# Hybrid decoder trunk: another order for the planned work behind the attention, from a planner that takes VectorE and GpSimd to share a port

## The chip, the cores and the metric

One core of a Trainium2 chip. The time is device microseconds of one execution. TensorE (PE) does the matmuls and the transposes, VectorE (DVE), ScalarE (ACT) and GpSimd (POOL) the rest; SyncE (SP) issues most loads and stores. Each engine runs its own queue in order and waits on semaphores of the others.

## The reference

One layer on x of 1024 tokens by 1024 channels, all in float32:

```python
h = rms_norm(x, norm1_g)
q, k, v, glu_a, glu_b = split(h @ w_in)          # 512 channels each
attn = stick_breaking_attention(norm(q), norm(k), v)   # 8 heads of 64
c = silu(layer_norm(causal_depthwise_conv(glu_a * sigmoid(glu_b))))   # width 31
x = x + concat([attn, c]) @ w_out
h = rms_norm(x, norm2_g)
gate, val = split(h @ w_up)                      # 2816 channels each
x = x + (silu(causal_depthwise_conv3(gate)) * val) @ w_down
```

## The kernel before

A float32 operand is split in two: a high part rounded to fp32r and a low part, the difference. A product is three matmuls per 128 channels: high by high, high by low, low by high (mm3, lines 289 to 291). Making an operand so takes a cast (ACT) and a subtraction (DVE or POOL).

The kernel has four parts. The first, some 450 us, is the input projection, the conv branch and the attention, with the conv's share of the output projection (op, lines 1200 to 1231) strewn between the attention's matmuls. The second, which the change rewrites, is the rest of the output projection, the second norm and the preparation of the up projection, 450 to 534 us. Then come the up projection (22 blocks of 128 channels of gate and of value) and the down projection.

The up projection uses a block scheme with seven products instead of eight. It treats tokens 0 to 511 and 512 to 1023, and channels 0 to 511 and 512 to 1023, as a 2 by 2 matrix of blocks: 11, 21 (first half of the tokens), 22, and sums of blocks T1 to T4, each in a high and a low part (B, names b11, b21, b22 and bT1 to bT4). The weights are treated alike: a11, a12, a22 and sums S1 to S4 (names a and aS).

In the second part there are eight tiles of 128 tokens, taken in the order 0, 4, 1, 5, 2, 6, 3, 7. For a tile, the steps are (function tokens, from line 1318):

- m: the attention's output of the tile in two parts, on ACT and DVE or POOL (L1332 to L1340).
- two products opa of twelve matmuls each, of 512 output channels (mm3), and each one's add to x on DVE (L1353); x is stored for the down projection.
- the sum of squares on ACT (L1363), its root on POOL (rstd, L280 and L281), and h, the normalized row, in two halves on DVE (L1371).
- two groups of four transposes of h on PE (h2T, L1379).
- for tiles 0 to 3 the copies raws and the blocks 11 and 21; for tiles 4 to 7 the differences t1 to t4 against the tile four before, the block 22, and T1 to T4. A block's part is a cast on ACT (L1391) and a subtraction on DVE or POOL (L1392).

The operands of the first up block (function first_operands, L1500 to L1511) are made at the same time; its weights are rawu. When all this is there, the up products run (up, from line 1531).

The order of parts one and two comes from a planner (class Plan, line 46): every step is an Op with a cost in ns per engine that may run it, a key (a due time) and its predecessors. Plan.run emits in a loop the step that could start first: a step whose key is at most 1 above the lowest open key is ranked by its start less PATIENCE, then by its key. The engine queues are tied to that order. Parts three and four, and the first operands' successors, are ordered by the framework's scheduler, which may set instructions of part three between planned ones. Parts one and two are two plans with the same rules.

In the second part's plan h has key + 0.5, the transposes + 0.7, all blocks + 1.0, and everything else the tile's own number; the first operands come from key FIRST = 7.0.

Of the kernel before, what the change touches and what calls it, by code (L numbers as in the profile page):

```python
# [34 lines left out]
ORDERED = (mybir.EngineType.PE, mybir.EngineType.DVE, mybir.EngineType.Activation, mybir.EngineType.Pool)  # L35
HORIZON, PATIENCE = 3.0, 200
AHEAD_Z, AHEAD_SCAN = 1.7, 0.9
QK_FROM, QK_TO = -3.0, 7.0
CONV_FROM, CONV_TO = 7.0, 31.0
EARLY = 4.0  # L40
W_SHIFT = 0.5
WA_FROM = 30.5
FIRST = 7.0
N_DN = 20


class Plan:
# [8 lines left out]
    class Op:  # L56
        __slots__ = ("cost", "emit", "key", "after", "takes", "end", "engine", "n", "kb")

# [21 lines left out]
    def add(self, cost, *args):  # L80
        if not isinstance(cost, dict):
            cost, args = {cost: args[0]}, (lambda eng, f=args[1]: f(),) + args[2:]
        op = Plan.Op()
        op.cost, op.emit, op.key = cost, args[0], args[1]
        op.after = list(args[2]) if len(args) > 2 else []
        op.takes = list(args[3]) if len(args) > 3 else []
        op.end, op.engine, op.n, op.kb = None, None, len(self.ops), 512
        self.ops.append(op)
        return op
# [17 lines left out]
    def run(self, busy):  # L107
# [12 lines left out]
        left = {id(t): len(set(o.n for o in t.users)) for t in self.tokens}  # L120
        done, dma = 0, 0.0
        main = sorted(self.ops, key=lambda op: op.key)
        low = 0
        while done < len(self.ops):
# [4 lines left out]
            for op in ready:  # L129
# [7 lines left out]
                for e, cost in op.cost.items():  # L137
                    r = room
                    for o in op.after:
                        r = max(r, o.end + (0 if o.engine == e else Plan.POOL_HAND_OVER if e == "POOL" else Plan.HAND_OVER)  # L140
                                + (170 if o.engine == "PE" and e != "PE" else 0))
                    start = max(r, at[e])
                    if e == "SP":
                        start = max(start, dma - 2000)
                    if mine is None or start + cost < mine[0]:
                        mine = (start + cost, e, cost, start)
# [11 lines left out]
            op.end, op.engine = start + cost, e  # L158
            at[e] = (start + 60) if e == "SP" else op.end - over[e]
            if e == "SP":  # L160
                dma = max(dma, start) + op.kb * 2.6
            op.emit(e)
# [14 lines left out]
def kernel(  # L177
# [1135 lines left out]

    ops_done = []

    raws = {}

    def tokens(t, key):
# [10 lines left out]
        def m_high():  # L1329
# [5 lines left out]
        adds = []  # L1335
        a = add("ACT", 250, m_high, key, [], [mr])
        b = [add({"DVE": 260, "POOL": 460}, lambda eng: (nc.vector if eng == "DVE" else nc.gpsimd).tensor_tensor(
            d["m"][:, 1, 3], attn[1][:, tok], f32(d["m"][:, 0, 3]), op=ALU.subtract), key, [a])]
        a = add("ACT", 480, lambda: nc.scalar.copy(d["m"][:, 0, :3], attn[0][:, :, tok]), key, [a])
        b += [add({"DVE": 560, "POOL": 1000}, lambda eng: (nc.vector if eng == "DVE" else nc.gpsimd).tensor_tensor(  # L1340
            d["m"][:, 1, :3], attn[0][:, :, tok], f32(d["m"][:, 0, :3]), op=ALU.subtract), key, [a])]
        for nn in range(2):
# [9 lines left out]
            ops_done.append(m)  # L1352
            f = add("DVE", 690, lambda nn=nn, cols=cols: nc.vector.tensor_tensor(d["x"][:, cols], d["ps", nn], d["x"][:, cols], op=ALU.add), key, [m, xl])  # L1353
            mr.users += [m]
# [9 lines left out]

        c = add("ACT", 1100, square, key + 0.5, adds, [hr, r])
        f = add("POOL", 750, lambda: rstd(d["rs"], d["sq"], 1.0 / D), key + 0.5, [c])
        b = []
        for nn in range(2):
            cols = slice(nn * 512, (nn + 1) * 512)
            z = plan.token("z")  # L1370
            f = add("DVE", 690, lambda nn=nn, cols=cols: nc.vector.scalar_tensor_tensor(  # L1371
                d["h"][:, cols], d["x"][:, cols], d["rs"], g2[1 + nn], op0=ALU.mult, op1=ALU.mult), key + 0.5, [f] + g2_ready)
            r.users += [f]
# [6 lines left out]

            m = add("PE", 440, turn, key + 0.7, [f], [z])
            hr.users += [m]
# [3 lines left out]
        ends = []  # L1386
        key += 1.0
        either = {"DVE": 700, "POOL": 1330}

        def both(name, src, after, lows, raw=None):  # L1390
            a = add("ACT", 600, lambda: nc.scalar.copy(B[name][0][where], src()), key, after)  # L1391
            e = add(lows, lambda eng: (nc.vector if eng == "DVE" else nc.gpsimd).tensor_tensor(  # L1392
                B[name][1][where], (raw or src)(), f32(B[name][0][where]), op=sub), key, [a] + (copies if raw else []))
            ends.append(e)
            return [a, e]

        if t < NT // 2:
# [9 lines left out]
            for nn, (m, z) in enumerate(b):  # L1407
                z.users += [copies[nn]] + both(("11", "21")[nn], lambda nn=nn: d["b", nn], [m], {"POOL": 1330}, lambda nn=nn: raws[t][:, nn])[:1]
            raws["ready", t] = vr, copies, ends
# [14 lines left out]
        z2.users += [d2, d3] + both("22", lambda: d["b", 1], [m2], {"DVE": 690})  # L1424
        d4 = add("POOL", 1330, lambda: nc.gpsimd.tensor_tensor(d["t4"], d["t4"], d["t2"], op=sub), key, [d2] + before)
        both("T2", lambda: d["t2"], [d2], either)
        both("T1", lambda: d["t1"], [d1], either)
        both("T3", lambda: d["t3"], [d3], either)
        both("T4", lambda: d["t4"], [d4], either)
        vr.users += ends + [d4]  # L1430
# [39 lines left out]

    for n, t in enumerate((0, 4, 1, 5, 2, 6, 3, 7)):
        tokens(t, float(n))
    A = {}

    def first_operands(key):
# [19 lines left out]
        def both(name, of, after, k):  # L1495
            def high():
                t = (op.tile([P, 2, 4, P], F32R, tag="m", name=f"a{name}_0", bufs=1) if name == "22" else
                     whl([P, 2, 4, P], F32R, f"a{name}_0"))
# [3 lines left out]

            a = add("ACT", 620, high, key + k, after + ops_done)
            return [a, add({"DVE": 700, "POOL": 1330}, lambda eng: (nc.vector if eng == "DVE" else nc.gpsimd).tensor_tensor(
                A[name][1], src(of), f32(A[name][0]), op=ALU.subtract), key + k, [a])]

        def total(dst, x, y, op_, after, k):
# [4 lines left out]

            return [add({"DVE": 700, "POOL": 1330}, emit, key + k, after)]

# [9 lines left out]
        s4 = total("a12", "a12", "a11", ALU.subtract, s2 + e12, 0.5)  # L1524
        both("S4", "a12", s4, 0.5)

    first_operands(FIRST)
# [3 lines left out]
    def up(f, A):  # L1531
        def product(a, b):
            ps = (pso.tile([P, 512], F32, tag="bank", name=f"u{f}_{a}") if a in ("11", "12") else
                  psz.tile([P, 512], F32, tag="z", name=f"u{f}_{a}"))
            (ah, al), (bh, bl) = A[a], B[b]
            for k in range(4):
                mm3(ps, ah[:, k, :], al[:, k, :], bh[:, k, :], bl[:, k, :], k == 0, k == 3)
            return ps

# [195 lines left out]
```

## Time and profile before

| what | us |
|---|---|
| three runs | 1159.65, 1164.59, 1164.76 (median 1164.59) |
| profiled execution | 1164.32 |
| its span, first to last instruction | 1162.3 |
| PE busy | 1115.9 |
| DVE, ACT, POOL busy | 908.5, 649.6, 605.9 |
| mean granted clock of PE | 0.985 |

A row of the timeline holds start, duration, engine, line, operation, output and inputs with their sizes, the count of merged instructions, and in brackets the idle time ahead of it with what ended it. A group's row holds busy time and the mean of one in ns. A row of waits holds the sum, the count and the longest. A window's row holds its length, then for PE, weight loads, DVE, ACT and POOL the busy time and the instructions, the granted clock as a share, the share of DMA time and GB/s.

### The profile page before, as it was taken

The page shows a single profiled execution, that of the slowest core. Times are in us where ns is not written, and L with a number is a line of the kernel's source. Part 1 is how long each engine was busy: PE and PEld are TensorE (multiplying, and loading weights), DVE is VectorE, ACT ScalarE, POOL GpSimd, SP SyncE. Part 2 cuts the span into 40 slices and gives each one's busy share as a digit, 9 for nine tenths or more (in the row PEclk, how much of TensorE's full clock was granted, in tenths as well). Part 3 has the DMA queues.
Part 4 walks back from the last instruction along what each step waited for, and adds up shares of the span by engine and source line. Part 5 has one row for each costly group of instructions (what it writes and reads, how often), then busy time and mean ns, then how long its engine had stood idle before and what let it go on. Part 6 is the DMA issues. An engine that isn't in the chain of part 4 may idle for free.

```text
span 1162.3 us, 15965 instructions
## 1 busy us (share of the span) xinstructions
PE 1115.9 (96%) x5639; PEld 934.8 (80%) x5639; DVE 908.5 (78%) x1215; ACT 649.6 (56%) x1338; POOL 605.9 (52%) x516
## 2 busy tenths in 40 slices
PE   7999999988899998879999999999999999999998
PEld 5888899867788886668888888888888877888887
DVE  5399966569989887778798777777677689887886
ACT  6255698697777785543344343434333475766670
POOL 5077747567676653454433332233313176877880
PEclk8999999999999999979999999999999999999999
DMA  8011203121933105332422322222222462144303
GB/s 275 19 56 37 61 14 82 47 97 52 284 122 118 55 37 192 116 127 55 127 91 81 101 72 91 73 91 73 91 88 75 134 247 81 65 145 145 127 19 145
DMA packets 108637, 116.48 MB, mean 100 GB/s; under 512 B 20782, under 2 KB 88590, under 8 KB 108558
## 3 DMA queue, kind: packets, MB, share of 16 engines
q1 hardware_dynamic: 108414, 114.95, 30.3%
q8 instruction: 44, 0.72, 0.2%
q10 hardware_dynamic: 144, 0.52, 0.1%
q14 instruction: 35, 0.29, 0.1%
HBM read 82.95 MB, written 28.31 MB: 96 GB/s over the span
## 4 chain that ended last, share of the span: by engine, by line
PE 83%; DVE 7%; ACT 3%; DMA 3%; issue 1%; POOL 1%; SPq 0%; DVEq 0%; ACTq 0%
PE dn L1694 15%; PE u_S L291 7%; PE u_S L289 7%; PE u_S L290 7%; PE u L290 5%; PE u L291 5%; PE u L289 5%; PE po L1120 3%; PE wT L1092 2%; PE v L290 1%; PE v L289 1%; PE v L291 1%; PE glu_b L289 1%; PE glu_b L290 1%; PE glu_a L289 1%
## 5 line engine op out<-in xcount | busy, mean ns | idle before, releaser
L1694 PE MATMUL dn<-wd,wd 128*128 128x512 f32 x924 | 214.2, 393 | 4.3 <-DVE c L1697 2.9
L1694 PEld LDWEIGHTS dn<-wd,wd 128*128 128x128 f32 x924 | 173.7, 189 | 44.7 <-DVE c L1697 5.3
L1697 DVE TENSOR_TENSOR c<-dn,c 128x512 f32<-128x512 f32 x144 | 95.5, 683 | 17.7 <-PE dn L1694 17.3
L1601 ACT CAST wd<-rawd 128x512 fp32r<-128x512 f32 x154 | 87.4, 618 | 36.3 <-DMA rawd<-act_d 11.7
L1071 POOL TENSOR_TENSOR wt<-wt,nb 128x128 f32<-128x128 f32 (+3 forms) x64 | 78.2, 1223 | 50.0 <-DVE nb L1068 34.8
L291 PE MATMUL u_S<-bT,aS 128*128 128x512 f32 x264 | 102.8, 389 | 0.0
L290 PE MATMUL u_S<-bT,aS 128*128 128x512 f32 x264 | 102.7, 389 | 0.0
L289 PE MATMUL u_S<-bT,aS 128*128 128x512 f32 x264 | 102.5, 389 | 0.0
L1068 DVE TENSOR_TENSOR_SCAN nb<-nb,one 128x128 f32<-128x128 f32 (+3 forms) x64 | 85.4, 1345 | 8.6 <-ACT nb L1049 8.4
L285 ACT CAST aS<-rawu 128x512 fp32r<-128x512 f32 x63 | 38.8, 620 | 94.7 <-PE u_S L291 64.8
L1602 DVE TENSOR_TENSOR wd<-whole,wd 128x512 fp32r<-128x512 f32 x110 | 73.9, 684 | 16.7 <-ACT wd L1601 12.9
L1600 ACT COPY whole<-rawd 128x512 f32<-128x512 f32 x110 | 63.2, 584 | 36.6 <-DMA rawd<-in_w_down_dram 19.6
L1460 POOL TENSOR_TENSOR s<-rawu 128x512 f32<-128x512 f32 x21 | 30.8, 1466 | 98.6 <-DMA rawu<-in_w_up_dram 97.3
L1466 POOL TENSOR_TENSOR rawu<-rawu 128x512 f32<-128x512 f32 x21 | 29.0, 1380 | 81.7 <-DVE a L286 81.7
L289 PE MATMUL u<-b,a 128*128 128x512 f32 x176 | 69.9, 398 | 0.4 <-ACT b L1391 0.4
L290 PE MATMUL u<-b,a 128*128 128x512 f32 x176 | 69.7, 396 | 0.1
L291 PE MATMUL u<-b,a 128*128 128x512 f32 x176 | 69.5, 395 | 0.0
L1602 POOL TENSOR_TENSOR wd<-rawd,wd 128x512 fp32r<-128x512 f32 x44 | 57.4, 1322 | 12.1 <-ACT wd L1601 12.1
L285 ACT CAST a<-rawu 128x512 fp32r<-128x512 f32 x63 | 38.9, 621 | 44.1 <-PE u_S L291 30.7
L1555 DVE SCALAR_TENSOR_TENSOR y<-gv,cols_a,y 128x1023 f32<-128x1023 f32 (+1 forms) x44 | 57.0, 1296 | 7.8 <-ACT y L1553 7.7
L286 DVE TENSOR_TENSOR aS<-rawu,aS 128x512 fp32r<-128x512 f32 x63 | 53.5, 851 | 8.3 <-ACT aS L285 8.0
L291 PEld LDWEIGHTS u_S<-bT,aS 128*128 128x128 f32 x264 | 49.6, 188 | 10.6 <-DVE aS L286 0.4
(311 smaller groups left out, 3343.3 us busy)
## 6 DMA issues: line engine op xcount, KB each, us to landing
rawu<-in_w_up_dram SPq DMA_DIRECT2D x44, 512.0 KB
act_d<-y SPq DMA_DIRECT2D x22, 512.0 KB
rawd<-act_d SPq DMA_DIRECT2D x22, 512.0 KB
rawd<-in_w_down_dram SPq DMA_DIRECT2D x22, 512.0 KB
rawo<-in_w_out_dram SPq DMA_DIRECT2D x8, 512.0 KB
m<-conv_d SPq DMA_DIRECT2D x16, 256.0 KB
xt<-in_x_dram SPq DMA_DIRECT2D x8, 512.0 KB
x_part<-xt SPq DMA_DIRECT2D x8, 512.0 KB
```

What stands on the lines that cost most here:

```text
L285: nc.scalar.copy(hi, src)
L289: nc.tensor.matmul(ps, a_hi, b_hi, start=first, stop=False)
L290: nc.tensor.matmul(ps, a_hi, b_lo, start=False, stop=False)
L291: nc.tensor.matmul(ps, a_lo, b_hi, start=False, stop=last)
L1068: nc.vector.tensor_tensor_scan(rev, rev, ones_of[0][:, :w], 0.0, op0=ALU.mult, op1=ALU.add)
L1071: nc.gpsimd.tensor_tensor(d["wt"][:, :w], d["wt"][:, :w], d["nb"][:, o + 1:S + 1], op=ALU.mult)
L1555: nc.vector.scalar_tensor_tensor(y[:, j:], g[:, :S - j], par("fw", (KF - 1 - j) * NF + f), y[:, j:], op0=ALU.mult, op1=ALU.add)
L1600: nc.scalar.copy(whole, src)
L1601: nc.scalar.copy(t[:, 0], src)
L1602: lo_engine.tensor_tensor(t[:, 1], whole, f32(t[:, 0]), op=ALU.subtract)
L1694: nc.tensor.matmul(ps, a[:, tok], b, start=first and m == 0, stop=last and m == 2, skip_group_check=True)
L1697: nc.vector.tensor_tensor(sums[c][s], ps, sums[c][s], op=ALU.add)
```

## The change

Four things, all in the planner or in what it is given.

1. Keys of the second part. The m step moves to the tile's number - 0.5, the adds to - 0.8, the norm to + 0.4; blocks stay at + 1.0, and the sums T1 to T4 with the difference t4 go to + 2.2. The first operands' key is 7.7.
2. The planner's rules, for both plans. PATIENCE is 150. A POOL step that starts while DVE holds the port that the planner takes them to share, or a step with two SBUF operands on DVE (marked DVE2) that starts while POOL holds it, is reckoned longer. Loads are reckoned one by one, with at most eight under way. CONV_FROM, the key from which the conv's products are due in the first plan, goes from 7.0 to 8.0.
3. The blocks 11 and 21 of tile 3 are subtracted by DVE straight from PSUM instead of by POOL from the copy.
4. The first two up products of the first block (11 and 12) become steps of the plan with key 7.6, and their operands lie in the buffer of the attention's output (tag attn), which the gate and value rows (gv) take afterwards.

```diff
-HORIZON, PATIENCE = 3.0, 200
+HORIZON, PATIENCE = 3.0, 150
...
-CONV_FROM, CONV_TO = 7.0, 31.0
+CONV_FROM, CONV_TO = 8.0, 31.0
...
-FIRST = 7.0
+FIRST = 7.7
+TOKENS = (0, 4, 1, 5, 2, 6, 3, 7)
+M_AT = -0.5
+ADD_AT = -0.8
+NORM_AT = 0.4
+TURN_AT = 0.7
+BLOCK_AT = 1.0
+SUM_AT = 2.2
+BEGIN_AT = 7.6
...
-                        start = max(start, dma - 2000)
+                        start = max(start, landed[-8]) if len(landed) > 7 else start
+                    if e == "POOL" or e == "DVE" and op.shares:
+                        cost += min(cost, max(0, holds["DVE" if e == "POOL" else "POOL"] - start))
...
+            if e == "POOL" or e == "DVE" and op.shares:
+
+                other = "DVE" if e == "POOL" else "POOL"
+                at[other] += min(op.cost[e], max(0, holds[other] - start))
+                holds[e] = op.end
...
-        key += 1.0
-        either = {"DVE": 700, "POOL": 1330}
+        last, key = key + SUM_AT, key + BLOCK_AT
+        either = {"DVE2": 700, "POOL": 1330}
...
-                z.users += [copies[nn]] + both(("11", "21")[nn], lambda nn=nn: d["b", nn], [m], {"POOL": 1330}, lambda nn=nn: raws[t][:, nn])[:1]
+                if t == TOKENS[-2] or t == 3:
+                    z.users += [copies[nn]] + both(("11", "21")[nn], lambda nn=nn: d["b", nn], [m], {"DVE": 690})
+                else:
+                    z.users += [copies[nn]] + both(("11", "21")[nn], lambda nn=nn: d["b", nn], [m], {"POOL": 1330}, lambda nn=nn: raws[t][:, nn])[:1]
...
-        both("T2", lambda: d["t2"], [d2], either)
+        both("T2", lambda: d["t2"], [d2], either, key=last)
...
+                if name in ("11", "12") and "first" not in d:
+                    d["first"] = mixp.tile([P, 2, 2, 4, P], F32R, tag="attn", name="a_first")
...
+        for e, a, b in ((e11, "11", "11"), (e12, "12", "21")):
+            add("PE", 2730, lambda a=a, b=b: begun.update({a: product_up(0, A, a, b)}), BEGIN_AT, e + block_done[b], [plan.token("o")])
```

Three places show what the planner makes of it. Line numbers are those of each kernel: L1392 before is L1417 now, L1371 is L1396, L1353 is L1378, L1420 to L1422 are L1449 to L1451.

DVE, from the first transposes of tile 4 to h of tile 1 (h2_1), before:

```order
L1420 TENSOR_TENSOR raws0_5045<-h2T4_0_5089,raws0_5045 128x512
L1422 TENSOR_TENSOR t2_4_5107<-h2T4_1_5099,t2_4_5107 128x512
L1392 TENSOR_TENSOR b22_4927<-h2T4_1_5099,b22_4927 128x4x128
L1421 TENSOR_TENSOR t1_4_5106<-h2T4_1_5099,raws0_5045 128x512
L1392 TENSOR_TENSOR bT1_4929<-raws0_5045,bT1_4929 128x4x128
L1392 TENSOR_TENSOR bT3_4931<-t2_4_5107,bT3_4931 128x4x128
L1392 TENSOR_TENSOR bT2_4928<-t1_4_5106,bT2_4928 128x4x128
L1371 SCALAR_TENSOR_TENSOR h2_1_5128<-x2_1_4964,rs2_1_5127,g2_0_4966 128x512
L1392 TENSOR_TENSOR bT4_4930<-raws0_5045,bT4_4930 128x4x128
L1371 SCALAR_TENSOR_TENSOR h2_1_5128<-x2_1_4964,rs2_1_5127,g2_1_4982 128x512
```

and now:

```order
L1449 TENSOR_TENSOR raws0_5043<-h2T4_0_5087,raws0_5043 128x512
L1417 TENSOR_TENSOR bT1_4929<-raws0_5043,bT1_4929 128x4x128
L1450 TENSOR_TENSOR t1_4_5112<-h2T4_1_5128,raws0_5043 128x512
L1451 TENSOR_TENSOR t2_4_5113<-h2T4_1_5128,t2_4_5113 128x512
L1417 TENSOR_TENSOR b22_4927<-h2T4_1_5128,b22_4927 128x4x128
L1378 TENSOR_TENSOR x2_5_5026<-opa5_0_5097,x2_5_5026 128x512
L1396 SCALAR_TENSOR_TENSOR h2_1_5121<-x2_1_4945,rs2_1_5120,g2_0_4979 128x512
L1378 TENSOR_TENSOR x2_5_5026<-opa5_1_5133,x2_5_5026 128x512
L1396 SCALAR_TENSOR_TENSOR h2_1_5121<-x2_1_4945,rs2_1_5120,g2_1_4981 128x512
```

Three of the four bT subtractions stood before the first or the second half of h; now one does, and the adds of tile 5 (x2_5) stand there instead. On PE, a product of tile 5 now stands between the two groups of transposes of tile 4, and its second product and tile 2's first ahead of tile 1's transposes.

DVE, from the transposes of tile 6 to h of tile 3 and the adds of tile 7, before:

```order
L1420 TENSOR_TENSOR raws2_5300<-h2T6_0_5355,raws2_5300 128x512
L1422 TENSOR_TENSOR t2_6_5367<-h2T6_1_5361,t2_6_5367 128x512
L1421 TENSOR_TENSOR t1_6_5366<-h2T6_1_5361,raws2_5300 128x512
L1392 TENSOR_TENSOR b22_4927<-h2T6_1_5361,b22_4927 128x4x128
L1392 TENSOR_TENSOR bT1_4929<-raws2_5300,bT1_4929 128x4x128
L1392 TENSOR_TENSOR bT3_4931<-t2_6_5367,bT3_4931 128x4x128
L1392 TENSOR_TENSOR bT2_4928<-t1_6_5366,bT2_4928 128x4x128
L1392 TENSOR_TENSOR bT4_4930<-raws2_5300,bT4_4930 128x4x128
L1371 SCALAR_TENSOR_TENSOR h2_3_5387<-x2_3_5221,rs2_3_5386,g2_0_4966 128x512
L1371 SCALAR_TENSOR_TENSOR h2_3_5387<-x2_3_5221,rs2_3_5386,g2_1_4982 128x512
L1353 TENSOR_TENSOR x2_7_5302<-opa7_0_5370,x2_7_5302 128x512
L1353 TENSOR_TENSOR x2_7_5302<-opa7_1_5397,x2_7_5302 128x512
```

and now (the first add of tile 7, not shown, stands just ahead, h of tile 7 just behind):

```order
L1396 SCALAR_TENSOR_TENSOR h2_3_5373<-x2_3_5220,rs2_3_5372,g2_0_4979 128x512
L1449 TENSOR_TENSOR raws2_5304<-h2T6_0_5377,raws2_5304 128x512
L1451 TENSOR_TENSOR t2_6_5393<-h2T6_1_5387,t2_6_5393 128x512
L1417 TENSOR_TENSOR b22_4927<-h2T6_1_5387,b22_4927 128x4x128
L1450 TENSOR_TENSOR t1_6_5392<-h2T6_1_5387,raws2_5304 128x512
L1378 TENSOR_TENSOR x2_7_5288<-opa7_1_5395,x2_7_5288 128x512
L1396 SCALAR_TENSOR_TENSOR h2_3_5373<-x2_3_5220,rs2_3_5372,g2_1_4981 128x512
L1417 TENSOR_TENSOR b11_4925<-h2T3_0_5417,b11_4925 128x4x128
L1429 COPY raws3_5425<-h2T3_1_5432 128x512
L1417 TENSOR_TENSOR bT2_4928<-t1_6_5392,bT2_4928 128x4x128
L1417 TENSOR_TENSOR b21_4926<-h2T3_1_5432,b21_4926 128x4x128
L1417 TENSOR_TENSOR bT4_4930<-raws2_5304,bT4_4930 128x4x128
```

Where the four bT subtractions of tile 6 stood ahead of both halves of h2_3, the first half of h2_3 is now ahead of the whole group, the second behind tile 7's second add; two of the bT subtractions have gone to POOL and two behind h2_3, and the blocks 11 and 21 of tile 3 are now on this queue.

POOL, at the program's start, from the first tile's root (rs) on; lo_v is the low part of the value weights, cpad a zeroed edge; before:

```order
L280 TENSOR_SCALAR rs0_201<-sq0_200 128x1
L281 TENSOR_TENSOR rs0_201<-rs0_201,expo_122 128x1
L439 TENSOR_TENSOR lo_v0_1_210<-raw_v0_1_196,hi_v0_1_209 128x1024
L280 TENSOR_SCALAR rs1_216<-sq1_215 128x1
L281 TENSOR_TENSOR rs1_216<-rs1_216,expo_122 128x1
L280 TENSOR_SCALAR rs2_223<-sq2_222 128x1
```

and now:

```order
L303 TENSOR_SCALAR rs0_207<-sq0_206 128x1
L304 TENSOR_TENSOR rs0_207<-rs0_207,expo_122 128x1
L562 MEMSET cpad0_222 128x2x15
L303 TENSOR_SCALAR rs1_225<-sq1_224 128x1
L304 TENSOR_TENSOR rs1_225<-rs1_225,expo_122 128x1
L303 TENSOR_SCALAR rs2_245<-sq2_244 128x1
```

The low part of the second half of the value weights (lo_v0_1) has left POOL for DVE, where it stands between the first and the second tile's normalization.

## What the change does to the time: the prediction

> **What bounds the kernel now.** I read the page's head first, then the chain that ended last, then busy time by stretches, then who waited for whom in the stretch that the change rewrites, then the timeline there.
>
> ```profile
> span 1162.3 us, 15965 instructions
> PE 1115.9 (96%) x5639; PEld 934.8 (80%) x5639; DVE 908.5 (78%) x1215; ACT 649.6 (56%) x1338; POOL 605.9 (52%) x516
> PE 83%; DVE 7%; ACT 3%; DMA 3%; issue 1%; POOL 1%; SPq 0%; DVEq 0%; ACTq 0%
> ```
>
> TensorE (PE) is the bound: 96% busy, 83% of the chain. The change takes no matmul away, so it can gain only time in which PE waits or runs slowly. Where is that? Stretches (core, then PE, PEld, DVE, ACT and POOL busy, then the granted clock):
>
> ```profile
> core 0: us, PE busy (x) PEld busy (x) DVE busy (x) ACT busy (x) POOL busy (x), PEclk, DMA share, GB/s
> 11.00:16.10 5.10, 2.03 (x9) 1.66 (x10) 1.94 (x3) 4.73 (x9) 4.76 (x5) 0.50 1.14 328
> 21.20:240.00 218.80, 218.78 (x1378) 197.23 (x1377) 161.99 (x222) 141.14 (x403) 131.93 (x124) 1.00 0.17 52
> 240.00:311.20 71.20, 58.56 (x349) 47.77 (x347) 59.10 (x79) 57.61 (x139) 47.40 (x48) 0.98 0.41 125
> 311.20:448.00 136.80, 131.00 (x838) 113.36 (x839) 123.34 (x152) 104.44 (x223) 86.89 (x72) 1.00 0.34 102
> ...
> 474.80:482.00 7.20, 5.55 (x21) 4.21 (x21) 3.46 (x6) 3.91 (x8) 5.17 (x6) 0.76 0.40 145
> 491.30:499.00 7.70, 5.10 (x19) 3.94 (x19) 4.38 (x6) 3.90 (x8) 4.71 (x6) 0.78 0.36 136
> 508.70:515.90 7.20, 2.00 (x9) 1.57 (x8) 6.63 (x7) 1.44 (x4) 3.57 (x3) 0.73 0.06 15
> 515.90:523.00 7.10, 7.00 (x17) 5.09 (x18) 6.61 (x9) 5.29 (x10) 4.36 (x4) 0.55 0.39 134
> ```
>
> From 21.2 to 240 PE is full. From 240 to 448 (attention) it is idle 12.6 + 5.8 = 18.4 us. Behind the attention there are three holes, each with a clock below 1, and the last is the worst: it empties PE just ahead of the up projection. PE's waits from 448 to 534:
>
> ```profile
> PE h2T L1379 <- DVE h L1371: 9.1, 5, 4.9
> ```
>
> All three holes are one wait: the transposes of the normalized rows (h2T) wait for DVE, which makes h late. What DVE did instead, over 455 to 516, and at the third hole:
>
> ```profile
> L1353 DVE TENSOR_TENSOR x<-opa,x 128x512 f32<-128x512 f32 x15 | 10.0, 685 | 14.3 <-PE opa L291 14.3
> L1371 DVE SCALAR_TENSOR_TENSOR h<-x,rs,g 128x512 f32<-128x512 f32 x14 | 9.9, 738 | 1.0 <-POOL rs L281 1.0
> L1392 DVE TENSOR_TENSOR bT<-t,bT 128x512 fp32r<-128x512 f32 x6 | 8.2, 1407 | 0.0
> L1392 DVE TENSOR_TENSOR bT<-raws,bT 128x512 fp32r<-128x512 f32 x6 | 7.2, 1193 | 0.0
> ...
> 514.80 0.59 ACT L1403 COPY raws<-h2T 128x512 f32<-128x512 f32 x1 [5.76 <-PE h2T L1379]
> ...
> 507.70 3.44 DVE L1392 TENSOR_TENSOR bT<-t,bT 128x512 fp32r<-128x512 f32 x2
> ...
> 507.19 1.74 POOL L1511 TENSOR_TENSOR s<-rawu 128x512 f32<-128x512 f32 x1
> 508.89 1.71 POOL L1504 TENSOR_TENSOR a<-rawu,a 128x512 fp32r<-128x512 f32 x1
> ...
> 533.32 1.29 POOL L1425 TENSOR_TENSOR raws<-raws,t 128x512 f32<-128x512 f32 x1 [12.84 <-DVE t L1421]
> ```
>
> The low parts of the block sums (bT) stood ahead of h in DVE's queue. While POOL works on SBUF operands they take 3.44 / 2 = 1.72 us, one POOL instruction's time, where an h takes 0.74 and an add to x 0.69 (in a row they start 0.6 apart). The old plan reckoned 0.70 for each.
>
> **The change, part by part.** The profiled execution took 1164.32 us, 0.27 below the median of the runs (1164.59); 2.0 us lie outside its span. I sum against 1164.32.
>
> *Sums last, the port known, other offsets.* In the new order DVE makes h of token tile 1 with one bT subtraction ahead of it, not three, and half the bT subtractions of tiles 5 and 6 go to POOL. A product is twelve matmuls, and a pair of transposes follows:
>
> ```profile
> 459.06 0.39 PE L289 MATMUL opa<-hio,m 128*128 128x512 f32 x1
> ...
> 461.79 1.03 PE L1379 MATMUL h2T<-ident_r,h 128*128 128x128 f32 x8
> 462.58 0.48 PE L289 MATMUL opa<-hio,m 128*128 128x512 f32 x1
> ```
>
> So a product takes 2.73 us and a pair 0.79. To be had are the waits, 9.1 + 0.4 (the first up product's, 0.36 below) = 9.5 us, and what the low clock cost: (1 - 0.76) x 7.2 = 1.7, (1 - 0.78) x 7.7 = 1.7, (1 - 0.55) x 7.1 = 3.2, and 0.9 for the cold pair below (1.94 against 1.03). That is 17.0 us.
>
> ```profile
> 475.90 0.63 PE L1379 MATMUL h2T<-ident_r,h 128*128 128x128 f32 x4 [0.97 <-DVE h L1371]
> 477.21 0.63 PE L1379 MATMUL h2T<-ident_r,h 128*128 128x128 f32 x4 [0.67 <-DVE h L1371]
> 477.71 0.62 PE L289 MATMUL opa<-hio,m 128*128 128x512 f32 x1
> 478.13 0.63 PE L290 MATMUL opa<-loo,m 128*128 128x512 f32 x1
> ...
> 513.62 1.94 PE L1379 MATMUL h2T<-ident_r,h 128*128 128x128 f32 x8 [4.86 <-DVE h L1371]
> 515.92 1.28 PE L289 MATMUL u<-b,a 128*128 128x512 f32 x2 [0.36 <-ACT b L1391]
> ...
> 527.50 0.60 PE L1379 MATMUL h2T<-ident_r,h 128*128 128x128 f32 x4
> ```
>
> What stays? I follow the new queues. Holes one and two: ahead of tile 1's transposes PE now has two products and a half pair more, and DVE's queue up to that h is eight instructions of about 0.6; it ends some 0.7 us before PE asks. By the same counting tiles 5, 2 and 6 come out 0.4 to 0.6 us early. The third hole shrinks but stays. Take the end of tile 3's second product as zero. Ahead of tile 3's second transposes PE has two products of tile 7, tile 6's pair and a half pair: 2 x 2.73 + 0.79 + 0.4 = 6.7 us. DVE must wait for tile 6's pair (ends at 3.5), take ACT's copy (0.6), do four instructions of tile 6 (2.4), then the add of tile 7 (0.7) and the second half of h (0.7): 8.0. PE waits 1.4. Then the first up product needs tile 3's part of block 11. Its cast stands on ACT behind a cast of the second half of the first w_up tile:
>
> ```profile
> 501.78 0.38 SPq L1482 DMA_DIRECT2D rawu<-in_w_up_dram  x1
> ```
>
> That load was issued as its buffer came free and was used at 507.19 (above): 5.4 us at most. In the new order the buffer is free at about 2.1, so the cast is at 7.5, two more ACT instructions end at 9.2, DVE's subtraction at 9.9, while PE is through its transposes at 8.5. If the load takes less, the wait is 0.3. I keep 2.5 us of waits of the 5.2, and 1.7 of clock as behind the second hole. The change puts h of tile 6 and 5 close to their dates; I take 2.5 us for one of them missed, as behind the first hole (0.97 of wait and most of 1.7 of clock; 0 to 4).
>
> *First two products ahead of the last transposes.* The timeline above shows that they already were: up products from 515.92, the last transposes at 527.50 and later. The scheduler behind the plan had put five products there. The edit therefore adds no cover: it puts the last pair behind two products instead of three and four. h of tile 7 stands on DVE right behind tile 6's bT4, and in this order it is ready before the second product ends. What is added is a wait: the operands 11 and 12 now lie in the buffer that the gate and value rows take next, so ACT's copy of the first product waits for the end of the second (2.73 us). Behind it on ACT stand a cast and the copy of the last transposes, so tile 7's sums start 1.2 us later. Three products (8.2 us) cover twelve DVE instructions; at 0.6 to 0.7 this just fits. I take 1.5 us lost (0 to 9, below).
>
> Middle: 17.0 - (2.5 + 1.7) - 2.5 - 1.5 = 8.8 us gained, bounds 2 and 15.
>
> *The plan's rules reach the first plan too.* Loads are modelled otherwise, PATIENCE is 150, the conv products start at 8.0. At the start, the second half of w_v's low part goes from POOL to DVE:
>
> ```profile
> 10.56 3.10 POOL L439 TENSOR_TENSOR lo_v<-raw_v,hi_v 128x1024 fp32r<-128x1024 f32 x1 [2.14 <-ACT hi_v L435]
> ...
> 11.68 0.19 ACT L395 ACTIVATION_READ_ACCUMULATOR attn_first<-x_q 128x1 f32 x1
> ...
> 14.02 0.55 POOL L281 TENSOR_TENSOR rs<-rs,expo 128x1 f32<-128x1 f32 x1
> 14.60 1.28 DVE L399 SCALAR_TENSOR_TENSOR x_q<-x_q,rs,attn 128x1024 f32<-128x1024 f32 x1 [3.16 <-POOL rs L281]
> ...
> 16.04 1.94 PE L408 MATMUL hT<-ident_r,x_q 128*128 128x128 f32 x8 [2.57 <-DVE x_q L399]
> ```
>
> The sum of squares of the second tile was there at 11.87; rs waited on POOL behind lo_v. Now rs ends at about 12.7, and DVE, busy with lo_v until 12.7, normalizes it till 14.0: PE starts at 14.1, not 16.04. PE is full from there to 240, so 1.9 us go, bounds 0 and 2.6.
>
> From 215 to 448 nearly every instruction of attention changes its place. One thing can be named:
>
> ```profile
> PE op L290 <- DVE w_hl L1178: 2.0, 2, 1.3
> ```
>
> The first conv products (op) stood as nine matmuls in one piece and waited for the weights' low parts. Now they come three at a time and later: I take these 2.0 us as gone. For the rest of the reshuffle no row shows a price: its bounds are -6 (a third of the 18.4 idle) and +6; I take zero.
>
> Sum: 1164.3 - 8.8 - 1.9 - 2.0 = **1151.6 us**. The up and down projections behind 534 keep their instructions, so I carry them over unchanged.
>
> **The rivals.**
>
> *The sums collide at the first S products* (same sign, small). Six of the twelve DVE instructions behind the last transposes have two SBUF operands. If POOL is busy all through, each takes 1.72 for 0.65: 6.4 us more, of which PE waits about 5.4, plus 3.2 of cold clock, less the 1.5 counted: 7.1 worse, 1158.7. For: POOL gets the next tiles' sums just there. Against: in the old run POOL had nothing to do for the 12.8 us before 533.32, the time in which these instructions fall.
>
> *Attention loses its filling* (slower). The op products are what fills PE between the attention's waits. The stretch 240 to 311, mostly without them, is idle 12.6 / 71.2 = 18%, the next 5.8 / 136.8 = 4%. If the later op products leave 311 to 448 as idle as the first stretch, that costs 0.135 x 136.8 = 18.5 us, and w_hl's 2.0 stay: 1164.3 - 8.8 - 1.9 + 18.5 = 1172.1. It decides from 10.7 us of new idle time. Against: the last op products still stand right before the last transposes of attention.
>
> *The change doesn't do what it says.* The real hand-overs undo the plan as before, and each hole is as long with another name: only the start is gained, 1162.4.
>
> *The clock follows another rule.* Rows: waits of 0.97 and 0.67 us were enough for matmuls 0.43 apart (477.71, 478.13) where 0.23 is usual. The Trainium skill ("TensorE: Matmul & The Clock Gate", Part 1) says that the clock falls only after an idle window of about 3.4 us; by that the two short waits would have cost no clock, and the trace disagrees. If short waits stay at full clock, the 1.7 kept above and some 1.6 of the missed tile's 2.5 go: 1148.3.
>
> **How the numbers follow.** Forecast 0.58; clock 0.05; S products 0.15 (half over the line); change does nothing 0.12; attention 0.10. A measurement of this kernel can tell about 0.5% from no change (its three runs lie 5.1 us apart), so faster is below 1158.8, slower above 1170.4. Faster: 0.58 + 0.05 + 0.08 = 0.71; same: 0.07 + 0.12 = 0.19; slower 0.10. The likeliest case alone: 1145 to 1158. The range takes in the S products and leaves out most of the last two cases: 1145 to 1161.
>
> **What would show it.** Right: PE's wait for h of 9.1 us falls to 2 to 4 us, with one hole left at tile 3; the clock is 1 around tiles 1 and 2; PE's second burst starts at 14 us. Wrong: a wait of the S products for bT above 3 us, more than 21 us of PE idle time between 240 and 448, or a first op product that still waits for w_hl.

## The result, and the profile after

Four runs of the changed kernel took 1142.7, 1144.87, 1145.23 and 1145.35 us, median 1145.05; the kernel before, with one more run on the same chip, 1163.47. The ratio is 0.9843 (95% interval 0.9815 to 0.9871): 18.4 us less, where 12.7 were forecast. The time lies just inside the range, 0.05 above its low end. The profiled execution is that of 1144.87 us.

The page's head, and the chain of what ended last, after:

```profile
span 1143.0 us, 15964 instructions
PE 1104.3 (97%) x5639; PEld 928.3 (81%) x5639; DVE 902.6 (79%) x1213; ACT 650.8 (57%) x1339; POOL 605.2 (53%) x517
PE 85%; DVE 6%; ACT 4%; DMA 2%; issue 1%; POOL 1%; SPq 0%; DVEq 0%; ACTq 0%; POOLq 0%
```

The same 5639 matmuls keep PE busy for 11.6 us less: nothing of the work went, but less of it ran at half clock (the mean granted clock is 0.995 in this execution, 0.985 before). To see where the time went I take, from the timelines, the start of the first qk product, of the first opa product and of the first dn product (down projection), and the end of the last dn. The lengths of the four stretches between them, in us:

| | start to qk | qk to opa (attention) | opa to dn (second part, up projection) | dn |
|---|---|---|---|---|
| before | 203.78 | 244.29 | 491.58 | 218.54 |
| after | 202.12 | 239.74 | 476.41 | 220.63 |
| difference | -1.66 | -4.55 | -15.17 | +2.09 |
| forecast | -1.9 | -2.0 | -8.8 | 0 |

The third stretch whole, before and then after (length, then PE's busy time):

```profile
448.07:939.65 491.58, 479.85 (x2106) 393.95 (x2105) 369.43 (x455) 198.42 (x307) 172.54 (x134) 0.98 0.31 103
441.86:918.27 476.41, 472.14 (x2106) 389.18 (x2105) 364.70 (x457) 198.68 (x306) 174.84 (x135) 1.00 0.32 106
```

PE's idle time in it fell by 7.5 us (11.7 to 4.3), and the same 2106 matmuls took 7.7 less at a granted clock of 1.00 and not 0.98: half of the 15.2 us is waits, half is clock.

Who PE waited for behind the attention, 441 to 540 us, after:

```profile
PE h2T L1404 <- DVE h L1396: 1.1, 1, 1.1
PE u_S L313 <- DVE bT L1417: 0.8, 1, 0.8
...
PE u L312 <- ACT b L1416: 0.3, 1, 0.3
PE u L313 <- DVE b L1417: 0.3, 1, 0.3
```

The wait for h is down from 9.1 us to 1.1. What is left of it stands at tile 3, and it ends where the prediction said, with the first up product's two waits behind it. PE's timeline there:

```profile
493.56 0.60 PE L1404 MATMUL h2T<-ident_r,h 128*128 128x128 f32 x4
495.28 0.63 PE L1404 MATMUL h2T<-ident_r,h 128*128 128x128 f32 x4 [1.12 <-DVE h L1396]
496.25 0.50 PE L312 MATMUL u<-b,a_first 128*128 128x512 f32 x1 [0.34 <-ACT b L1416]
497.06 0.47 PE L313 MATMUL u<-b,a_first 128*128 128x512 f32 x1 [0.32 <-DVE b L1417]
497.37 0.40 PE L314 MATMUL u<-b,a_first 128*128 128x512 f32 x1
```

From 497.06 on the starts are 0.23 to 0.31 apart, so the clock is at full rate behind the hole, and the stretches say the same (length, then busy time of PE, PEld, DVE, ACT and POOL, then the granted clock):

```profile
446.00:470.00 24.00, 23.47 (x111) 19.10 (x110) 16.46 (x27) 11.67 (x24) 9.94 (x15) 1.00 0.44 155
470.00:492.00 22.00, 22.00 (x115) 18.55 (x114) 18.41 (x29) 13.94 (x29) 15.36 (x17) 1.00 0.55 191
492.00:500.00 8.00, 6.22 (x30) 4.65 (x29) 6.30 (x11) 6.04 (x12) 4.40 (x5) 1.00 0.66 198
```

Before, the stretches of the three holes stood at 0.55 to 0.78. PE's waits over the whole execution after, of which these fall in the attention and the down projection:

```profile
PE dn L1730 <- DVE c L1733: 4.8, 4, 2.1
PE z L1062 <- ACT wt L1075: 2.8, 5, 1.2
PE dn L1730 <- DVE gv L1733: 2.5, 2, 1.6
PE op L313 <- DVE w_hl L1201: 2.4, 3, 1.5
...
PE wT L1115 <- DVE tl L1136: 1.0, 2, 0.7
...
PE qk L312 <- DVE qk L898: 0.9, 1, 0.9
```

The same view of the kernel before has:

```profile
PE wT L1092 <- DVE tl L1113: 3.8, 4, 1.5
PE dn L1694 <- DVE c L1697: 2.9, 2, 2.1
PE qk L289 <- DVE qk L875: 2.1, 1, 2.1
PE z L1039 <- ACT wt L1052: 2.1, 4, 1.2
```

The op products' wait for w_hl, which was to go, rose from 2.0 to 2.4. What shrank are the waits for tl (3.8 to 1.0) and for qk (2.1 to 0.9), which the prediction did not name.

### The profile page after: what moved, and what is told of

It reads as the page before. It is cut to its first block, busy times and chain, and to the rows that moved or that the text cites. A ratio compares the mean times of both kernels' runs of the same rounds, so it can differ in the third digit from the quotient of the medians.

```text
span 1143.0 us, 15964 instructions
## 1 busy us (share of the span) xinstructions
PE 1104.3 (97%) x5639; PEld 928.3 (81%) x5639; DVE 902.6 (79%) x1213; ACT 650.8 (57%) x1339; POOL 605.2 (53%) x517
## 4 chain that ended last, share of the span: by engine, by line
PE 85%; DVE 6%; ACT 4%; DMA 2%; issue 1%; POOL 1%; SPq 0%; DVEq 0%; ACTq 0%; POOLq 0%
PE dn L1730 17%; PE u_S L313 7%; PE u_S L314 7%; PE u_S L312 7%; PE u L314 5%; PE u L312 5%; PE u L313 5%; PE po L1143 3%; PE wT L1115 2%; DVE nb L1091 2%; PE v L312 1%; PE v L313 1%; PE v L314 1%; PE glu_b L312 1%; PE glu_a L312 1%
## 5 line engine op out<-in xcount | busy, mean ns | idle before, releaser
L1591 DVE SCALAR_TENSOR_TENSOR y<-gv,cols_a,y 128x1023 f32<-128x1023 f32 (+1 forms) x44 | 60.2, 1369 | 9.2 <-ACT y L1589 9.2
L312 PE MATMUL u<-b,a 128*128 128x512 f32 x168 | 65.5, 390 | 0.0
L314 PE MATMUL u<-b,a 128*128 128x512 f32 x168 | 65.5, 390 | 0.0
L313 PE MATMUL u<-b,a 128*128 128x512 f32 x168 | 65.4, 389 | 0.0
```

The lines of the kernel that those rows point to most:

```text
L312: nc.tensor.matmul(ps, a_hi, b_hi, start=first, stop=False)
L313: nc.tensor.matmul(ps, a_hi, b_lo, start=False, stop=False)
L314: nc.tensor.matmul(ps, a_lo, b_hi, start=False, stop=last)
L1591: nc.vector.scalar_tensor_tensor(y[:, j:], g[:, :S - j], par("fw", (KF - 1 - j) * NF + f), y[:, j:], op0=ALU.mult, op1=ALU.add)
```

## The experiments

Each was timed in up to six runs beside up to eleven of the kernel before on the same chip (median of before 1162.76 to 1162.82). The changed kernel's 1145.05 was timed beside 1163.47 for before, so a difference of 1 us between its time and a run's says little. The stretches are those of the one profiled execution, as above, which can lie off the median of its kernel: 4.6 us above it in e1, and below it by 3.4 in e7, 2.7 in e3 and 2.6 in e10.

| run | us | ratio to before, 95% | start to qk | attention | opa to dn | dn |
|---|---|---|---|---|---|---|
| e1_first_plan_only | 1154.68 | 0.9929 (0.9909 to 0.9950) | 202.81 | 239.60 | 490.96 | 220.02 |
| e2_second_plan_only | 1149.63 | 0.9890 (0.9868 to 0.9912) | 203.37 | 244.28 | 476.99 | 217.50 |
| e3_sums_at_one | 1155.44 | 0.9935 (0.9914 to 0.9955) | 202.31 | 239.65 | 487.02 | 217.83 |
| e4_port_unknown | 1144.64 | 0.9841 (0.9820 to 0.9863) | 202.10 | 239.66 | 478.49 | 218.72 |
| e5_not_begun | 1146.25 | 0.9855 (0.9832 to 0.9878) | 202.05 | 239.72 | 479.49 | 219.23 |
| e9_tile3_on_pool | 1149.43 | 0.9884 (0.9865 to 0.9904) | 201.96 | 240.23 | 481.80 | 218.70 |
| e10_before_sums_last | 1153.32 | 0.9916 (0.9894 to 0.9939) | 203.21 | 244.28 | 477.56 | 219.61 |
| e6_conv_from_7 | 1147.10 | 0.9866 (0.9844 to 0.9887) | 203.29 | 242.34 | 477.85 | 219.82 |
| e7_patience_200 | 1154.51 | 0.9927 (0.9903 to 0.9951) | 201.67 | 248.35 | 477.18 | 217.77 |
| e8_loads_as_before | 1149.21 | 0.9880 (0.9854 to 0.9905) | 204.17 | 243.11 | 477.42 | 220.26 |
| e11_conv_from_9 | 1147.29 | 0.9872 (0.9844 to 0.9900) | 202.35 | 243.34 | 476.26 | 218.65 |
| e12_h3_late | 1145.18 | 0.9852 (0.9828 to 0.9876) | 202.59 | 239.96 | 478.00 | 218.56 |

My theory after the result: the gain is two separate ones, one for each plan; in the second part it is the sums that had stood ahead of h; in the attention it is the new order as such. The rivals are in the expectations.

**The two plans apart.** e1 is the changed kernel with the old rules, keys and operands in part two; e2 the other way round.

```diff
 e1, second plan:
-    plan = Plan({"z": 4, ...
+    plan = PlanOld({"z": 4, ...
 e2, first plan:
-    plan = Plan({"s": 3, ...
+    plan = PlanOld({"s": 3, ...
```

> Part one planned by the new rules (PATIENCE 150, CONV_FROM 8, port, loads one by one), part two by the old keys, the old rules and old operands; DVE's order of part two is that of before. Theory A (the three stretches add up: start -1.4 to -1.8, attention -4.5, the rest belongs to part two's plan): start of the first opa product 6 us earlier than before, its h waits back at 8 to 10 us, the time 5 to 7 us below before, about 1157. Rival B (attention's gain is an accident of the whole program, of where the scheduler sets later work): the first opa product comes 2 us earlier or less, the time within 3 us of before. The down projection's new 2 us should not be there under A if part two's plan or the operands' new place makes them.

> Part one planned by the old rules, part two as in the changed kernel; DVE's order of part two is that of the changed kernel. Theory A (the stretches add up): first opa product at 448 as before, from there to the first down product 15 us less than before, down projection 2 us more, the time 12 to 15 us below before, about 1150. Rival B: the h waits depend on how part one ends (what is loaded and cast by then): h waits above 4 us, less than 9 us gained. Rival C (the forecast's middle term, 8.8): 8 to 9.5 us gained.

Measured: e1 8.1 us below before (a little more than the 5 to 7 expected), e2 13.1 below. Together that is 21.2 against 18.4 for the whole change, which the intervals allow. The attention keeps 239.60 with the new first plan whatever follows, and 244.28 with the old one; opa to dn is 476.99 with the new second plan and 490.96 with the old. So these two stretches add up (theory A), both rivals on the influence of one part on the other fall, and so does rival C of e2. e1's wait for h is back:

```profile
PE h2T L1523 <- DVE h L1515: 8.0, 5, 3.8
```

The expectation on the down projection fails: e1, with the old second plan, has 220.02, and e2, with the new one, 217.50. Over the fourteen profiled executions this stretch lies between 217.50 and 220.63 with either plan at both ends. The 2.1 us that it seems to lose are thus not shown to be the change's.

**What acts in the second part.** e10 gives the kernel before one new key, that of the sums; e3 takes that key from the changed kernel; e4 takes the port away from the planner; e9 undoes edit 3; e5 undoes edit 4.

```diff
 e10, on the kernel before:
-        key += 1.0
+        last, key = key + 2.2, key + 1.0
...
-        both("T2", lambda: d["t2"], [d2], either)
+        both("T2", lambda: d["t2"], [d2], either, key=last)
...
 e3:
-SUM_AT = 2.2
+SUM_AT = 1.0
 e4, both places:
-                    if e == "POOL" or e == "DVE" and op.shares:
+                    if False:
 e9:
-                if t == TOKENS[-2] or t == 3:
+                if False:
 e5:
-        for e, a, b in ((e11, "11", "11"), (e12, "12", "21")):
-            add("PE", 2730, lambda a=a, b=b: begun.update(...), BEGIN_AT, ...)
```

> The kernel before with one thing changed: the sums T1 to T4 and t4 due at the tile's number + 2.2. Everything else, the first plan too, is as before. Theory A (the sums ahead of h were the middle's loss, and moving them is enough): the wait for h falls from 9.1 us to under 3, first opa at 448, from there to the first down product 11 to 15 us less than before's 491.6, the time 1148 to 1152. Rival B (the earlier adds and m steps, the port or the planned products are needed too): the wait for h 4 to 7 us, the time 1154 to 1159.

Measured: the wait for h falls from 9.1 to 0.3, opa to dn is 477.56, 14.0 of the 15.2 us. Theory A holds. (The median is 9.5 below before, its time a little above the 1148 to 1152 expected, where the whole second plan, e2, gains 13.1. The profiled execution is the second fastest of its six, so the 14.0 is the key's worth in one good execution; by the medians it is 9.5, with an interval of 7.1 to 12.3.) What is left in the profile is mainly the first up product, which waits for POOL's low part of block 11 and others, with half clock behind:

```profile
PE u L290 <- POOL b L1392: 1.6, 1, 1.6
...
PE u L289 <- ACT b L1391: 0.8, 1, 0.8
```

> The changed kernel with the sums T1 to T4 and t4 due at the tile's number + 1.0 as before, not + 2.2; the other keys, the port and the begun products stay. In this order the four bT subtractions of tiles 4, 5 and 6 stand ahead of h of the next tile on DVE again. Theory A (sums ahead of h are what PE waited for): h waits of 6 to 10 us come back with a low clock behind them, the time 8 to 12 us above the changed kernel's 1145, about 1155. Rival B (the earlier adds and m steps have made enough room): h waits under 4 us and the time 1145 to 1149.

Measured: 10.4 us above the changed kernel, opa to dn 10.6 longer. The wait is back at the third hole, though not at the first two; there PE waits for DVE's adds to x, which free the PSUM banks of its products:

```profile
PE h2T L1404 <- DVE h L1396: 5.7, 2, 5.4
...
PE opa L312 <- DVE x L1378: 4.2, 2, 2.7
```

Theory A holds; its number for the wait for h, 6 to 10, is met only with the waits for x counted in.

> The changed kernel whose planner doesn't reckon a longer time for two steps on the shared port; keys, loads, PATIENCE and begun products stay, in both plans. Theory A (the order of keys does the work, port knowledge moves a few subtractions between DVE and POOL): the time 1145 to 1149, h waits up to 4 us. Rival B (without it DVE is given sums that take 1.7 us instead of 0.7 and h is late again): h waits above 6 us, 1150 to 1156.

Measured: 1144.64, the changed kernel's time. The keys do the work; that the plan knows the port is worth nothing that shows here. In the first plan it could not act: no step there is marked DVE2, so only the loads, PATIENCE and CONV_FROM differ in it. (One up product waits 1.68 for b there, with half clock behind, and opa to dn is 2.1 longer in that execution; in the median it does not show.)

> The changed kernel with edit 3 undone: tile 3's blocks 11 and 21 get their low parts from POOL out of the copy. Theory A (the third hole ends with this chain): the first up products' waits for b rise from 0.7 us to 2 to 3, the window of 3.4 us in which they fall goes below half busy, and with the low clock behind it the time is 3 to 5 us more, 1148 to 1150. Rival B (POOL is free just then): waits under 1.5 us, 1144 to 1147.

Measured: 4.4 us above the changed kernel, as theory A's sum has it, but only in part by its chain. The first up products' waits for b come to 1.3, not 2 to 3; half clock follows them, from 499.19 on. With the two subtractions gone to POOL, seven steps on weights of the up projection stand on DVE ahead of h of tile 7 (three of them slowed to 1.7 us), and its transposes wait 2.5, with half clock again from 509.43 on:

```profile
499.38 1.77 DVE L1550 TENSOR_TENSOR s<-rawu 128x512 f32<-128x512 f32 x1
...
503.12 3.48 DVE L309 TENSOR_TENSOR a<-rawu,a 128x512 fp32r<-128x512 f32 x2
...
507.12 1.39 DVE L1396 SCALAR_TENSOR_TENSOR h<-x,rs,g 128x512 f32<-128x512 f32 x2
```

```profile
508.01 0.63 PE L1404 MATMUL h2T<-ident_r,h 128*128 128x128 f32 x4 [2.50 <-DVE h L1396]
```

> The changed kernel without the two planned up products (edit 4 undone but for the operands' place); DVE's order up to h of tile 7 is the same, and on PE the framework's scheduler again sets products 11 and 12 ahead of tile 7's transposes. Theory A (the prediction's: the edit adds no cover): the wait for h about 1 us as in the changed kernel, first up product within 1 us of 496.3, the time 1143 to 1148. Rival B (the planned products change what the plan does with tile 7 and the operands, and so cover something): 3 to 6 us more, 1148 to 1151, as a wait of tile 7's transposes or of the S products.

Measured: 1146.25, 1.2 above the changed kernel, which e5's interval does not tell from none; the first up product starts at 497.41 (changed: 496.25), 0.1 past the 1 us expected, and the wait for h is 1.1. The scheduler again puts both products ahead of tile 7's transposes. Edit 4 adds no cover, as predicted. A wait of the S products for an operand (1.6 us, aS) takes the place of their wait for bT (0.8), and opa to dn is 3.1 longer in that execution.

**What acts in the first plan.** One rule each is put back (e6 CONV_FROM, e7 PATIENCE, e8 the loads), and CONV_FROM is moved on (e11).

```diff
 e6:
-CONV_FROM, CONV_TO = 8.0, 31.0
+CONV_FROM, CONV_TO = 7.0, 31.0
 e11:
+CONV_FROM, CONV_TO = 9.0, 31.0
 e7, first plan alone:
-                rank = (max(start - PATIENCE, at[e]), op.key) ...
+                rank = (max(start - (200 if self.first else PATIENCE), at[e]), op.key) ...
 e8, first plan alone:
-                        start = max(start, landed[-8]) if len(landed) > 7 else start
+                        start = max(start, dma - 2000) if self.first else max(start, landed[-8]) if len(landed) > 7 else start
...
-            if e == "SP":
+            if e == "SP" and self.first:
+                at[e] = start + 60
+                dma = max(dma, start) + op.kb * 2.6
+            elif e == "SP":
```

> The changed kernel with CONV_FROM at 7.0 again. The attention ran from the first qk product to the first opa product in 244.3 us before and 239.7 now. Theory A (the later conv products give attention its 4.6 us): 243 to 244.3 here, the time about 1149. Rival B (PATIENCE or the loads' reckoning gives it): 239 to 241, the time 1144 to 1147. The start, to the first v product at 16.3, stays in both.

Measured: attention 242.34, 2.6 of the 4.6 lost, the time 2.1 above the changed kernel. It lies between the two numbers.

> The changed kernel with PATIENCE 200 in the first plan alone (part two keeps 150). From the first qk to the first opa product: 244.3 before, 239.7 changed, 242.3 with CONV_FROM at 7. Theory A (the 2.0 that CONV_FROM leaves over are PATIENCE's): 241 to 242.3 here, the time 1 to 3 us above the changed kernel. Rival B (they are the loads'): 239.7 as changed, the time 1144 to 1146.

Measured: the attention takes 248.35, 4 us longer than before, and the median is 9.5 us above the changed kernel. Neither theory has that.

> The changed kernel whose first plan reckons loads as before (one stream, no count of loads under way). Theory A (the loads' reckoning is what moved the low part of the value weights to DVE at the start): PE's second burst at 16.0 again, not 14.7, the first v product at 17.6. From the first qk to the first opa product 239.7 if loads have no part in the attention's gain, 241 to 242 if they give its other 2.0. The time 1146 to 1149.

Measured: the start is as before. The low part of the value weights is back on POOL, ahead of rs, and PE's second burst (the transposes of its second tile) is late:

```profile
10.39 3.11 POOL L465 TENSOR_TENSOR lo_v<-raw_v,hi_v 128x1024 fp32r<-128x1024 f32 x1 [2.15 <-ACT hi_v L461]
13.58 0.19 POOL L306 TENSOR_SCALAR rs<-sq 128x1 f32<-128x1 f32 x1
```

```profile
15.88 0.87 PE L434 MATMUL hT<-ident_r,x_q 128*128 128x128 f32 x3 [2.58 <-DVE x_q L425]
```

So the loads' reckoning gives the start's gain. The attention is 243.11, 3.4 longer, past the 241 to 242 expected.

> The changed kernel with CONV_FROM at 9.0, one step further the same way. Theory A (the later the conv products, the better they fill the attention's waits): from the first qk to the first opa product 237 to 239, the time 1142 to 1144. Rival B (past 8 the op products are missing in the middle and pile up at the end): 240 to 243, the time 1146 to 1149.

Measured: attention 243.34: rival B. The op products then start at 314.1 instead of 306.1, and PE is busy for only 0.76 of the 3.41 us from 309.26.

Put back one at a time, the three rules lose 2.6, 8.6 and 3.4 us of a gain of 4.6. They do not add up, and a step on in the same direction loses 3.6. The order that the changed planner finds for the attention is good as a whole, and no rule carries the gain alone. These are attentions of one profiled execution each. It is reproducible, though: the kernels with this plan lie within 239.60 and 240.23, the three with the old one at 244.28 and 244.29.

**What a short hole costs.** e12 lengthens the third hole and nothing else in part two.

```diff
-            f = add("DVE", 690, lambda nn=nn, cols=cols: nc.vector.scalar_tensor_tensor(..., op1=ALU.mult), ...
+            f = add("DVE", 690, lambda nn=nn, cols=cols: [nc.vector.scalar_tensor_tensor(..., op1=ALU.mult)
+                for _ in range(3 if (t, nn) == (3, 1) else 1)], ...
```

> The changed kernel in which DVE makes the second half of h of tile 3 three times over (the same instruction, the same result): two instructions of 0.65 us more ahead of the third hole, nothing else moved in part two. In all runs so far a 3.41 us stretch of the clock's raster in which PE is busy under about half is followed by one at half clock. Theory A (so many waits in one such stretch bring the low clock): the wait for h 1.1 becomes 2.4, one or two stretches at clock 0.5 behind it, 3 to 5 us from the first opa to the first down product more than the changed kernel's 476.4. Rival B (short waits cost no clock, only 3.4 us without a break do): 1.3 us more and the clock 1.

Measured: the wait is 2.7 us and the clock falls behind it, as theory A says; rival B falls. But opa to dn grows by 1.6, not 3 to 5, and the median by 0.1, which cannot be told from none. PE's timeline:

```profile
497.90 1.09 PE L1405 MATMUL h2T<-ident_r,h 128*128 128x128 f32 x4 [2.69 <-DVE h L1396]
498.64 0.78 PE L312 MATMUL u<-b,a_first 128*128 128x512 f32 x1
499.21 0.63 PE L313 MATMUL u<-b,a_first 128*128 128x512 f32 x1
...
500.49 0.58 PE L313 MATMUL u<-b,a_first 128*128 128x512 f32 x1
500.91 0.40 PE L314 MATMUL u<-b,a_first 128*128 128x512 f32 x1
```

The first up product's two waits (0.34 and 0.32) have gone into the longer one, so the waits grew by 2.69 - 1.78 = 0.9, and of the slow 3.41 us only 3.0 had work in them. The two instructions of 0.65 thus added less than their length to the waits, because other waits stood right behind; with the half clock the stretch still grew by more than their 1.3.

## Why the prediction was right, and where it was not

**What bounded the kernel.** Right. The middle's loss was one wait, h behind the sums on DVE: e10 moves only the sums and gains 14.0 us of that stretch (9.5 by the medians), e3 moves them back and loses 10.6 (10.4). That it was the sums' place and not the plan's knowledge of the port is shown by e4; the prediction had taken both as one edit. (Of tile 4's bT subtractions, three stood ahead of the first half of h2_1 before and the fourth ahead of the second, so all four and not three stood ahead of one of its halves.) The other new keys were not tried apart. They and edits 3 and 4 stand between e10's 9.5 us and e2's 13.1, a difference that the intervals do not tell from none.

**The middle's size.** Too small: 8.8 forecast, 15.2 measured, just past the bound of 15. The 17.0 us to be had agree with the rows of the whole stretch. Of what was to stay, 8.2, there remained 1.12 + 0.34 + 0.32 + 0.76 = 2.5, which leaves 14.5; of the 0.7 beyond that, by those rows, 0.5 is idle time elsewhere in the stretch and 0.2 busy time. The terms that were mis-sized: the third hole's 2.5 of waits is 1.8; its 1.7 of clock is 0 in the profiled execution (the other three runs have no profile); the 2.5 for one missed tile did not come, and no tile's h but tile 3's is late; the 1.5 at the S products is 0.8. The third hole itself was worked out nearly right: 1.4 forecast for h and 1.12 measured. The load ahead of block 11 took 5.1 us, near the 5.4 that the prediction allowed at most:

```profile
489.48 0.38 SPq L1519 DMA_DIRECT2D rawu<-in_w_up_dram  x1
...
494.60 0.62 ACT L1539 CAST a<-rawu 128x512 fp32r<-128x512 f32 x1 [1.26 <-DMA rawu<-in_w_up_dram]
```

Even so the wait for block 11 is 0.66 and not 1.4: the first matmul (at 496.25) needs only the cast, and PE does it while DVE makes the low part. Edit 3 was not priced at all: e9 gives it 4.4 us beside the other edits, while e10, which lacks it, is only 0.6 longer in this stretch than e2.

**The clock.** The step that failed is that any hole of a microsecond brings the low clock. It depends on how much of a fixed stretch of 3.41 us is empty. The changes of the granted clock lie on such a raster; here the two steps of it around the second and third holes before, with PE's busy time in the first column after the length:

```profile
491.58:494.99 3.41, 0.99 (x8) 0.81 (x8) 3.41 (x5) 1.70 (x4) 2.03 (x3) 1.00 0.00 0
494.99:498.41 3.42, 3.42 (x11) 2.63 (x10) 0.69 (x2) 2.12 (x4) 2.34 (x4) 0.50 0.73 277
508.65:512.06 3.41, 0.11 (x1) 0.00 (x0) 3.41 (x3) 0.39 (x1) 3.41 (x3) 1.00 0.00 0
512.06:515.47 3.41, 1.85 (x8) 1.57 (x8) 3.27 (x5) 0.67 (x2) 0.21 (x1) 0.50 0.02 6
```

and the third hole after, then with the longer wait of e12:

```profile
492.98:496.39 3.41, 1.94 (x13) 1.33 (x11) 2.31 (x5) 2.15 (x5) 3.41 (x3) 1.00 0.54 174
496.39:499.80 3.41, 3.10 (x13) 2.34 (x14) 3.01 (x5) 2.83 (x6) 0.63 (x3) 1.00 0.70 195
```

```profile
494.04:497.46 3.42, 1.17 (x8) 0.76 (x6) 3.35 (x6) 2.16 (x5) 3.42 (x3) 1.00 0.56 197
497.46:500.87 3.41, 2.97 (x9) 2.58 (x10) 2.69 (x5) 1.94 (x4) 0.17 (x1) 0.50 0.57 172
```

A stretch with 1.94 us of work keeps the clock, one with 1.17 halves it for the next. The fourth rival (short waits cost no clock, 1148.3) is nearest to the time measured, but not its rule: the wait in e12 is 2.7 us, shorter than 3.4, and the clock fell. The Trainium skill ("TensorE: Matmul & The Clock Gate", Part 1) says that the activity window is 3413 ns and free-running; the raster agrees. The Trainium skill calls the window ahead of the fall idle; here a window with 1.17 us of work in it was enough.

**The start.** Right in its cause (e8): lo_v left POOL. Its size is 1.7 of 1.9. PE's second burst is at 14.68, not 14.1, because the root took 1.3 us on POOL (0.68 and 0.56) and DVE waited 0.73 for it:

```profile
11.89 0.68 POOL L303 TENSOR_SCALAR rs<-sq 128x1 f32<-128x1 f32 x1 [3.46 <-ACT attn_first L418]
12.65 0.56 POOL L304 TENSOR_TENSOR rs<-rs,expo 128x1 f32<-128x1 f32 x1
...
13.25 1.28 DVE L422 SCALAR_TENSOR_TENSOR x_q<-x_q,rs,attn 128x1024 f32<-128x1024 f32 x1 [0.73 <-POOL rs L304]
```

**The attention.** Wrong in its reason. The wait for w_hl did not go, as "What would show it" named for a sign of error, and yet the stretch gained 4.6, more than double the 2.0. The gain comes from the reshuffle that the prediction bounded at -6 and +6 and set to zero; e6, e7, e8 and e11 show that it turns on the three rules together. Which instruction's new place carries it stays open.

**Edit 4.** Right: no cover added (e5). The wait feared for the S products came to 0.8 us.

**The rivals.** The S products' collision did not come (0.8 us). The attention did not lose its filling, though e7 shows how near that case lay: one number set back costs it 8.6 us against the changed kernel, 4.1 against before. That the change does nothing is excluded by the interval.

**The total.** The wait and its cure were understood, the sizes were not: the middle gave 6.4 us more than forecast and the attention 2.6 more, from a term set to zero, and a down projection 2.1 longer in the profiled execution, counted as 0, set off a part. That the total still falls inside the range, by 0.05 us, is luck.

## What to carry to other kernels

When one engine's queue makes another wait, look for work in that queue whose result nobody needs yet, and give it a later due time: one key was worth 9.5 us here by the medians (14.0 of the 15.2 in the profiled executions), and the finer model of the port nothing that shows. Count a hole on PE with what else stands empty in the same 3.41 us: below about half busy (49%) the next 3.41 us ran at half clock, above 58% a hole cost only its length. A planner's constants act on the whole order, so try each alone and both ways before giving one of them the gain.

## What the runs showed of the hardware

Over the fourteen profiled executions, from 10 to 1135 us, there are 4504 whole stretches of the raster at full clock, 45 of them followed by one at half clock. Of those in which PE was busy 1.66 us or less (49%) each was followed by one at half clock; of those with 1.98 or more (58%) none; in between both occurred. The way back needs more: at half clock a stretch with 3.15 us or more always led to full clock, one with 2.73 or less never. The raster is not tied to the start of the span: the clock first falls to half at 10.32 us before and at 11.73 after, which are not a multiple of 3.41 apart. So a hole of 1.5 to 3 us can cost clock in one run and, I expect, none in the next. The four runs of the changed kernel agree with that: their mean granted clocks are 0.995, 0.996, 0.989 and 0.988 (at 1144.87, 1142.7, 1145.23 and 1145.35 us). I take this for a part of the runs' spread, which no run here separates; but it can't cost its full length: by my estimate, 0.008 of 1143 us is 18 us more at half clock, 9 us if PE were the bound throughout, and the times lie 2.7 apart. Half clock cost nothing that shows where PE isn't the bound: e1 has three such stretches between 252 and 262 us, the changed kernel one, and their attention is 239.60 and 239.74.
